# Making two of the four weight sums of a column pair in accumulating DMAs

## The chip, the cores and the metric

The kernel runs on one core of a Trainium2 chip. The metric is the device time of one execution in microseconds. The engines are TensorE (PE in the profile, with its weight loads as PEld), VectorE (DVE), ScalarE (ACT), GpSimd (POOL) and SyncE (SP), which only issues DMAs. GpSimd issues DMAs as well. Each engine runs its instructions strictly in the order of the program.

## The reference

One layer of a hybrid network on 640 tokens (128 of context, 512 latent): a SwiGLU feed-forward half step, a mixer (bidirectional mLSTM and a gated short convolution), and a second half step, all in float32. Cut to the large products:

```python
h = modulate(rmsnorm(x, norm_g[0]), sh1, sc1)
x = x + 0.5 * g1 * swiglu(h, ffn1_w1, ffn1_w2)     # w1: 1024 x 5632, w2: 2816 x 1024
h = modulate(rmsnorm(x, norm_g[1]), shm, scm)
y, C, n, m = mixer(h, C0, n0, m0, ...)             # h @ w_in: 1024 x 9232, then three 1024 x 1024
x = x + gm * y
h = modulate(rmsnorm(x, norm_g[2]), sh2, sc2)
x = x + 0.5 * g2 * swiglu(h, ffn2_w1, ffn2_w2)

def swiglu(h, w1, w2):
    a, b = jnp.split(h @ w1, 2, axis=-1)
    return (jax.nn.silu(a) * b) @ w2
```

## The kernel before

**Exact products.** A float32 operand is split into a rounded high part and the rest: `split` (L75, L79) makes `wh` on ScalarE by a cast and `wl` on VectorE by a subtraction. A product is three matmuls (`three`, L245 to L247): high by high, high by low, low by high, each 128 x 128 weights by 320 tokens.

**Column pairs.** Most large products go two columns of 128 outputs at a time, for the two halves of the tokens (320 each) and the two halves of the inner dimension (512 each). That is a 2 x 2 product of blocks, made with seven products instead of eight in Winograd's form. The seven take the weight operands A11, S1, S2, A12, S3, S4, A22 in this order, with the sums

S1 = A21 + A22, S2 = S1 - A11, S3 = A11 - A21, S4 = A12 - S2.

Of a block Aij, i is the column and j the half of the inner dimension. Each of the seven multiplies by an activation operand of its own, which is kept split as well: 11, T1, T2, 21, T3, 22, T4, in tiles named H11, HT1 and so on, or U where they are made inside the feed-forward. One product is 4 x 3 matmuls. There are 81 pairs. `pair_steps` issues the products and the evacuations between them; among these is the copy of S2's result in PSUM to another bank by ScalarE (L290), where S3's product is then accumulated; VectorE adds partial results (L301).

**Weights.** SP loads the two columns of a pair with one 512 KB DMA each (`w_load`, L202) into the ring `wr` of five tiles. `cast_more` then makes the sums into the ring `ws` (four tiles, L218) and the split operands into the rings `wh` and `wl` (six each), up to four operands ahead of TensorE. The four sums are VectorE's, except that in ten pairs of the mixer (`cx_pair` and `bg_pair`, argument `e1`) S1 and S3 are GpSimd's. A tile of `wr` is free for the next load when its last block is cast (`rdone`).

**The feed-forward** takes its hidden columns in groups of 6 or 8; after each group the product with w2 is added to x. In the second feed-forward two of the groups are "eights": the activation tiles HT3 and HT4 are lent to the hidden values, saved before in DRAM (`h_away`, to `hd`) and read back behind the group's use (`h_back`: 16 DMAs of 160 KB on GpSimd, HT3 before HT4, L981). Each waits until TensorE has read the lent tile for the last time. In between, x itself goes to DRAM and back by `x_away` (L969) and `x_back` (L966), on GpSimd too.

**Order.** The order on each engine is that in which the Python code issues; nothing reorders it. Work for GpSimd stands in its queue wherever a step of the program puts it. A DMA of SP or GpSimd takes one of eight semaphores in turn, and waits until the DMA that used it before has landed.

Of the kernel before, what the change touches and what calls it, by code (L numbers as in the profile page):

```python
# [7 lines left out]
F32 = mybir.dt.float32  # L8
# [36 lines left out]
def mixer_step(ctx: ExitStack, tc: tile.TileContext, x_prompt, x_sample, state_C, state_n, state_m,  # L45
# [33 lines left out]
            V.tensor_sub(lo, raw, f32(hi))  # L79


    RAWB, OPB, SB, AHEAD = 5, 6, 4, 4
    raws, ops = [], []
    rtile, optile, rdone = {}, {}, set()
    ptr = {"dma": 0, "sum": 0, "cast": 0, "use": 0, "held": 0, "hold": False, "cap": 1 << 20}
    fill = []

    def drain(left=0):
        while len(fill) > left:
            fill.pop(0)["emit"]()  # L90

    def load_more(upto=1 << 20):
        while ptr["dma"] < min(upto, len(raws)) and (ptr["dma"] < RAWB or ptr["dma"] - RAWB in rdone):
            n = ptr["dma"]
            rtile[n] = ring.tile([P, 1024], F32, name="wr", bufs=RAWB)
            raws[n](rtile[n])
            ptr["dma"] += 1

    def ready(op):
        return all(r < ptr["dma"] for r in op["raws"])  # L100

    def cast_more(upto):
        load_more()
        while ptr["cast"] < min(upto, ptr["held"] + OPB, ptr["cap"], len(ops)):
            n = ptr["cast"]
            if not ready(ops[n]):
                return
            while ptr["sum"] < min(n + 2, len(ops)) and ready(ops[ptr["sum"]]):
                o = ops[ptr["sum"]]
                o["ap"] = o["src"](o)  # L110
                ptr["sum"] += 1
            o = ops[n]
            w = o["n"]
            hi = ring.tile([P, 512], F32R, name="wh", bufs=OPB)
            lo = ring.tile([P, 512], F32R, name="wl", bufs=OPB)
# [84 lines left out]
    def w_load(w, row0, nk, col0, ncol):  # L200
        def load(t):
            nc.sync.dma_start(t[:, :nk * P].rearrange("p (k n) -> p k n", k=nk),  # L202
                              dap(w, row0 * ncol + col0, [[ncol, P], [P * ncol, nk], [1, P]]))
        return load


# [1 line left out]

    LH, RH = slice(0, 512), slice(512, 1024)

    def pair_ops(r1=0, r2=1, e1=None):
        e1 = e1 or V

        def total(key, engine, fn, a, b):
            def src(o):
                g = o["group"].setdefault(r1, {})
                t = g[key] = ring.tile([P, 512], F32, name="ws", bufs=SB)
                getattr(engine, fn)(t, part(o, a), part(o, b))  # L218
                return t
            return src  # L220

        def part(o, key):
            if key[0] == "S":
                return o["group"][r1][key]
            return rtile[o["base"] + (r1 if key[1] == "1" else r2)][:, LH if key[2] == "1" else RH]

        whole = lambda key: lambda o: part(o, key)
        spec = lambda src, *r: {"raws": list(r), "n": 512, "src": src}
        return {
            "A11": spec(whole("A11"), r1), "A12": spec(whole("A12"), r1), "A22": spec(whole("A22"), r2),  # L230
            "S1": spec(total("S1", e1, "tensor_add", "A21", "A22"), r2),
            "S2": spec(total("S2", V, "tensor_sub", "S1", "A11"), r1, r2),
            "S3": spec(total("S3", e1, "tensor_sub", "A11", "A21"), r1, r2),
            "S4": spec(total("S4", V, "tensor_sub", "A12", "S2"), r1, r2),
        }

    ACT_OF = {"A11": "11", "A12": "21", "A22": "T4", "S1": "T1", "S2": "T2", "S3": "T3", "S4": "22"}
# [29 lines left out]
    def pair_steps(order, ev, spare_v, acts):  # L267
        S = {}

        def prod(name, ps, start):  # L270
            hi, lo = op()
            for kk in range(4):
                three(ps[:, :HT], hi, lo, kk, acts[ACT_OF[name]][kk], start and kk == 0, kk == 3)

        for name in order:
            if name == "A11":
                S["a"] = big()
                prod(name, S["a"], True)
                S["b"] = big()
                A.copy(S["b"][:, :HT], S["a"][:, :HT])  # L280
                flush()
            elif name == "S1":
                e = big()
                prod(name, e, True)
                S["p5"] = t3()
                A.copy(S["p5"], e[:, :HT])
            elif name == "S2":
                prod(name, S["b"], False)
                S["c"] = big()
                A.copy(S["c"][:, :HT], S["b"][:, :HT])  # L290
            elif name == "A12":
                prod(name, S["a"], False)
                ev(0, 0, S["a"][:, :HT])
            elif name == "S3":
                prod(name, S["c"], False)
                S["c22"] = t3()
                if spare_v:
                    A.copy(S["c22"], S["c"][:, :HT])
                    V.tensor_add(S["c22"], S["c22"], S["p5"])
                else:  # L300
                    V.tensor_add(S["c22"], S["c"][:, :HT], S["p5"])  # L301
            elif name == "S4":
                prod(name, S["b"], False)
                V.tensor_add(S["p5"], S["b"][:, :HT], S["p5"])
                ev(0, 1, S["p5"])
            else:
                prod(name, S["c"], False)
                late.append(lambda: ev(1, 0, S["c"][:, :HT]))
                late.append(lambda: ev(1, 1, S["c22"]))
            yield  # L310

    def pair_el(load1, load2, ev, e1=None, spare_v=False, acts=HB, at=None, calm=False):
        po = pair_ops(e1=e1)
# [10 lines left out]
        return dict(element([load1, load2], [po[name] for name in ORDER], emit), pair=True)  # L324

    def tile_ops(nk, t=0):
        out = []
# [565 lines left out]
    def right_chain(n, sh):  # L893
# [26 lines left out]
            V.tensor_sub(N["T", k], N[1, k], N[0, k])  # L920

        def t2(k):
            V.tensor_sub(N["T", k], N[1, k + 4], N["T", k])

        def t3_(k):
            V.tensor_sub(N[1, k], N[1, k + 4], N[1, k])

        def t4(k):
            V.tensor_sub(N["T", k], N[0, k + 4], N["T", k])
# [53 lines left out]
    def eights(w1, w2, g, f0, n_head, head, more, back):  # L983
# [24 lines left out]
        def ev_of(j):  # L1008
            sa, k = {}, j % 4

            def left():
                put_own("11", k, sa[0])

            def diff1():
                V.tensor_sub(raw2(k), raw3(k), sa[0])
                put_own("T1", k, raw2(k))

            def diff2():
                V.tensor_sub(raw2(k), sa[1], raw2(k))
                put_own("T2", k, raw2(k))  # L1020

            def diff3():
                put_own("21", k, sa[0])
                V.tensor_sub(raw3(k), sa[1], raw3(k))

            def diff4():
                put_22(k, sa[1])
                V.tensor_sub(raw2(k), sa[0], raw2(k))

            def ev(mi, h, src):  # L1030
                if mi == 0:
                    sa[h] = raw3(k) if h and j < 4 else t3()
                    A.activation(sa[h], src, AF.Silu)
                    return
                V.tensor_mul(sa[h], src, sa[h])
                if h == 0:
                    if j < 4:
                        lazy.append(left)
                else:
                    lazy.extend([diff1] if j < 4 else [diff2, diff3, diff4])  # L1040
            return ev
# [33 lines left out]
                               spare_v=True, acts=UB, at=at))  # L1075
        return grp, w2s

    def ffn(w1, w2, g, lists, head_of, n_head, e1=None, groups=(6, 6, 6, 4), more={}):

        head, els, f0 = [], [], 0  # L1080
        for gi, size in enumerate(groups):
# [6 lines left out]
            for j in range(size):  # L1088
# [14 lines left out]
                if f0 + j < n_head:  # L1103
                    head.extend(blocks_of(p))
                else:
                    grp.append(pair_el(*p, e1 if f0 == 0 else None, at=more.get(gi, {}).get(j)))
# [777 lines left out]

    h0 = head_q(0)
    chain, work = right_chain(1, SHM)
    prog.append(head_el(blocks_of(h0[0]) + blocks_of(h0[1]), chain, work, mod_mid(GM, 0), gate_rows))
    def tanh_first():
        A.activation(tp.tile([P, 3], F32, name="rstd", bufs=2)[:, 0:1], eps, AF.Tanh)

    prog += [step(spill_x), step(halve), step(tanh_first)]
    cols, gate, NG = gate_cols(), gates(), 22
    h1 = head_q(1)
    first_gml = pair_el(*gml_pair(0), spare_v=True)
# [141 lines left out]
    prog += with_units(ml, mod_dve(GM, (1,), m_wide) + mod_dve(SH2, (1,), m_wide))  # L2036
    for m in range(0, KT, 2):
        if m:
            prog += [pair_el(*cx_pair(m), G), pair_el(*cx_pair(m + 1), G)]
        prog.append(pair_el(*bg_pair(m), G, spare_v=True))  # L2040
# [136 lines left out]
```

## Time and profile before

| | |
|---|---|
| runs | 1652.0, 1652.42, 1652.5 us; median 1652.42 |
| profiled execution | 1651.78 us; its span 1649.9 us |
| TensorE busy | 1628.9 us (99%), 11093 matmuls, granted clock 0.999 |
| VectorE, ScalarE, GpSimd busy | 1319.5 us (80%), 826.4 us (50%), 223.3 us (14%) |
| weight sums | 304 on VectorE (0.684 us each), 20 on GpSimd (1.299 us) |
| DRAM | read 188.98 MB, written 25.79 MB |

The profile is of one execution. A row of the timeline gives the start, the duration, the engine, the line, and the operation with output<-input; in brackets stands how long the engine was idle before it and what released it. Instructions of one engine overlap in the pipeline, so that the distance between two starts is shorter than a duration. A row of the DMA list gives the queue, the number of DMAs, their size and the median time from issue to landing.

### The profile page before, as it was taken

Reading aid. Unit: us, or ns where it says so; the run is one execution under the profiler, and the core shown is the slowest. Engines: PE = TensorE matmul, PEld = TensorE weight load, DVE = VectorE, ACT = ScalarE, POOL = GpSimd, SP = SyncE. Lnnn points to the kernel's source line nnn. Section 1 sums busy time; section 2 is a strip of 40 time slices with the busy share of each in tenths; the row PEclk is TensorE's granted clock in tenths of the full one; section 3 lists DMA queues with packets and bytes.
Section 4 is the critical chain, followed back from the end, with each engine's and each line's share of the span. In section 5 each row is a group of like instructions: output and inputs, shape, how many; then the busy total and the mean of one; then the engine's idle time right before and its main releaser. Section 6 shows DMA issues by size and latency. Waiting matters only on the chain.

```text
span 1649.9 us, 29478 instructions
## 1 busy us (share of the span) xinstructions
PE 1628.9 (99%) x11093; PEld 1585.9 (96%) x11093; DVE 1319.5 (80%) x2786; ACT 826.4 (50%) x1805; POOL 223.3 (14%) x354
## 2 busy tenths in 40 slices
PE   8999999999999999999999999999999999999998
PEld 5999999999999999999999999999999999999997
DVE  6867887887778878788897899779688897898765
ACT  5642542542566655465561455633275555564443
POOL 2010000000031321221121221011112012003002
PEclk9999999999999999999999999999999999999999
DMA  9454343343353433342258432357355256337522
GB/s 321 116 165 120 105 128 112 103 125 94 114 172 102 102 101 90 84 118 71 84 180 263 113 90 78 106 169 222 117 166 141 84 178 175 88 117 219 172 81 64
DMA packets 283661, 216.68 MB, mean 131 GB/s; under 512 B 9331, under 2 KB 260602, under 8 KB 283520
## 3 DMA queue, kind: packets, MB, share of 16 engines
q1 hardware_dynamic: 263152, 158.36, 33.4%
q0 software_dynamic: 20336, 56.45, 11.5%
q8 instruction: 87, 1.43, 0.4%
q14 instruction: 54, 0.44, 0.1%
q10 hardware_dynamic: 32, 0.01, 0.0%
HBM read 188.98 MB, written 25.79 MB: 130 GB/s over the span
## 4 chain that ended last, share of the span: by engine, by line
PE 89%; DVE 4%; ACT 3%; DMA 2%; issue 1%; POOL 0%; SPq 0%; ACTq 0%; DVEq 0%
PE ps L245 27%; PE ps L246 27%; PE ps L247 27%; PE ax L1717 2%; PE ax L1748 2%; PE ax L1720 1%; DVE wl L79 1%; ACT wh L75 1%; ACT Uh L867 1%; DMA early<-in_w_mod_dram 1%; DMA HT4l<-hd 1%; PE ax L1694 1%; DMA wr<-in_ffn_w_dram 0%; ACT Uh L75 0%; DVE Uh L859 0%
## 5 line engine op out<-in xcount | busy, mean ns | idle before, releaser
L79 DVE TENSOR_TENSOR wl<-wr,wh 128x512 fp32r<-128x512 f32 (+1 forms) x389 | 261.4, 684 | 79.8 <-ACT wh L75 77.5
L75 ACT CAST wh<-wr 128x512 fp32r<-128x512 f32 (+1 forms) x391 | 230.2, 600 | 89.1 <-PE ps L246 69.3
L79 DVE TENSOR_TENSOR wl<-ws,wh 128x512 fp32r<-128x512 f32 x324 | 228.0, 704 | 39.5 <-ACT wh L75 38.7
L75 ACT CAST wh<-ws 128x512 fp32r<-128x512 f32 x324 | 199.0, 620 | 108.9 <-DVE ws L218 71.4
L245 PE MATMUL ps<-Uh,wh 128*128 128x320 f32 x576 | 179.8, 312 | 0.0
L246 PE MATMUL ps<-Ul,wh 128*128 128x320 f32 x576 | 177.9, 309 | 0.2
L247 PE MATMUL ps<-Uh,wl 128*128 128x320 f32 x576 | 177.7, 309 | 0.0
L245 PE MATMUL ps<-HT4h,wh 128*128 128x320 f32 x408 | 128.5, 315 | 0.2 <-DVE t L301 0.2
L246 PE MATMUL ps<-HT4l,wh 128*128 128x320 f32 x408 | 126.3, 309 | 0.5 <-DMA HT4l<-hd 0.4
L247 PE MATMUL ps<-HT4h,wl 128*128 128x320 f32 x408 | 126.0, 309 | 0.0
L245 PE MATMUL ps<-H11h,wh 128*128 128x320 f32 x376 | 118.8, 316 | 0.7 <-ACT H11h L75 0.7
L245 PE MATMUL ps<-H21h,wh 128*128 128x320 f32 x376 | 117.7, 313 | 0.0
L246 PE MATMUL ps<-H11l,wh 128*128 128x320 f32 x376 | 116.5, 310 | 0.3
L247 PE MATMUL ps<-H21h,wl 128*128 128x320 f32 x376 | 116.2, 309 | 0.0
L247 PE MATMUL ps<-H11h,wl 128*128 128x320 f32 x376 | 116.1, 309 | 0.0
L246 PE MATMUL ps<-H21l,wh 128*128 128x320 f32 x376 | 116.0, 308 | 0.0
L245 PE MATMUL ps<-HT3h,wh 128*128 128x320 f32 x356 | 112.0, 315 | 3.5 <-ACT ps L290 3.5
L246 PE MATMUL ps<-HT3l,wh 128*128 128x320 f32 x356 | 110.0, 309 | 0.0
L247 PE MATMUL ps<-HT3h,wl 128*128 128x320 f32 x356 | 110.0, 309 | 0.0
L245 PEld LDWEIGHTS ps<-Uh,wh 128*128 128x128 f32 x576 | 108.1, 188 | 1.4 <-issue 0.8
L246 PEld LDWEIGHTS ps<-Ul,wh 128*128 128x128 f32 x576 | 108.1, 188 | 0.7 <-DVE Ul L79 0.7
L247 PEld LDWEIGHTS ps<-Uh,wl 128*128 128x128 f32 x576 | 108.1, 188 | 0.0
(477 smaller groups left out, 4699.4 us busy)
## 6 DMA issues: line engine op xcount, KB each, us to landing
wr<-in_ffn_w_dram SPq DMA_DIRECT2D x102, 512.0 KB, 3.9
wr<-in_w_in_dram SPq DMA_DIRECT2D x72, 512.0 KB, 3.9
wr<-in_w_mod_dram SPq DMA_DIRECT2D x51, 512.0 KB, 3.9
wr<-in_ffn_w_dram SPq DMA_DIRECT2D x32, 384.0 KB, 3.3
xd<-x POOLq DMA_DIRECT2D x32, 320.0 KB, 5.4
x<-xd POOLq DMA_DIRECT2D x32, 320.0 KB, 4.0
early<-in_w_mod_dram SPq DMA_DIRECT2D x13, 512.0 KB, 9.0
mg<-in_w_mod_dram POOLq DMA_DIRECT2D x8, 512.0 KB, 5.6
```

Of the source, the lines that this page charges most:

```text
L75: A.copy(hi, raw)
L79: V.tensor_sub(lo, raw, f32(hi))
L245: PE.matmul(ps, hi[:, ws], ah, start=start, stop=False, skip_group_check=True)
L246: PE.matmul(ps, hi[:, ws], al, start=False, stop=False, skip_group_check=True)
L247: PE.matmul(ps, lo[:, ws], ah, start=False, stop=stop, skip_group_check=True)
L867: A.activation(t[:, a:b], t[:, a:b], AF.Identity, scale=sc_, bias=bi_)
L1694: PE.matmul(p[:, :P], S["k", dt][:, sl], S["q", dt][:, sl], start=(dt == 0), stop=(dt == 1))
L1717: PE.matmul(p2[:, :DH + 1], S["q", dt][:, sl], S["C"][d][:, dt, :], start=(dt == 0), stop=(dt == 1))
L1720: PE.matmul(p1[:, :DH + 1], S["p", ch][:, d, :], PO["vt"][:, ch, :], start=True, stop=True)
L1748: PE.matmul(p[:, :DH + 1], kw[:, dt * P:(dt + 1) * P], PO["vt"][:, ch, :], start=True, stop=True)
```

## The change

S1 = A21 + A22 and S3 are no longer computed by an engine. For each pair SP loads the block A21 twice, into the two halves of a `wr` tile (`sums`), then the first column (A11, A12) as before, then the block A22 into a new ring `wq` of two half-size tiles (`last`). GpSimd then issues two DMAs with `accum_op=add` (`more`): A22 onto one copy of A21, which makes S1, and A11 onto the other, which makes S3 = A11 + A21. Each waits for the landing of its plain copy. `add_more` emits them, at the start of the next `cast_more`, or just ahead of a sum that needs them. For this S3 has to be a sum; so signs change elsewhere: S2 = S1 + A11 and S4 = A12 + S2, the activation operands T2 and T3 are negated and T4, made from T2, adds it, VectorE subtracts S4's result where it added it, and the copy of S2's result (L290) becomes a ScalarE activation with scale -1. S2 and S4 stay on VectorE; the ring `ws` shrinks to two tiles. The argument `e1` is gone. The step `spill_x` (DMAs of x to DRAM) moves ahead of the head element of the mixer.

```diff
-    RAWB, OPB, SB, AHEAD = 5, 6, 4, 4
+    RAWB, HALFB, OPB, SB, AHEAD = 5, 2, 6, 2, 4
...
+    turns, accs = {"wr": [], "wq": []}, []
...
     def load_more(upto=1 << 20):
-        while ptr["dma"] < min(upto, len(raws)) and (ptr["dma"] < RAWB or ptr["dma"] - RAWB in rdone):
+        while ptr["dma"] < min(upto, len(raws)):
             n = ptr["dma"]
-            rtile[n] = ring.tile([P, 1024], F32, name="wr", bufs=RAWB)
+            kind = getattr(raws[n], "kind", "wr")
+            seq, bufs = turns[kind], RAWB if kind == "wr" else HALFB
+            if len(seq) >= bufs and seq[-bufs] not in rdone:
+                return
+            seq.append(n)
+            rtile[n] = ring.tile([P, 1024 if kind == "wr" else 512], F32, name=kind, bufs=bufs)
             raws[n](rtile[n])
+            if hasattr(raws[n], "more"):
+                accs.append((n, raws[n].more))
             ptr["dma"] += 1
+
+    def add_more(n=1 << 20):
+
+        while accs and accs[0][0] <= n:
+            r, f = accs.pop(0)
+            f(rtile[r])
...
     def cast_more(upto):
+        add_more()
         load_more()
...
+                add_more(max(o["raws"]))
...
-    def pair_ops(r1=0, r2=1, e1=None):
...
+    def pair_loads(load1, load2):
+
+        def quad(t, o, load, half, queue, **kw):
+            w, row0, col0, ncol = load.src
+            queue.dma_start(t[:, 512 * o:512 * o + 512].rearrange("p (k n) -> p k n", k=4),
+                            dap(w, (row0 + 512 * half) * ncol + col0, [[ncol, P], [P * ncol, 4], [1, P]]), **kw)
+
+        def sums(t):
+            for o in (1, 0):
+                quad(t, o, load2, 0, nc.sync)
+
+        def more(t):
+            quad(t, 1, load2, 1, G, accum_op=OP.add)
+            quad(t, 0, load1, 0, G, accum_op=OP.add)
+
+        def last(t):
+            quad(t, 0, load2, 1, nc.sync)
+        sums.more = more
+        last.kind = "wq"
+        return [sums, load1, last]
...
-            "S1": spec(total("S1", e1, "tensor_add", "A21", "A22"), r2),
-            "S2": spec(total("S2", V, "tensor_sub", "S1", "A11"), r1, r2),
-            "S3": spec(total("S3", e1, "tensor_sub", "A11", "A21"), r1, r2),
-            "S4": spec(total("S4", V, "tensor_sub", "A12", "S2"), r1, r2),
+            "A11": spec(whole("A11"), 1), "A12": spec(whole("A12"), 1), "A22": spec(whole("A22"), 2),
+            "S1": spec(whole("S1"), 0), "S3": spec(whole("S3"), 0),
+            "S2": spec(total("S2", "S1", "A11"), 0, 1),
+            "S4": spec(total("S4", "A12", "S2"), 1),
...
-                A.copy(S["c"][:, :HT], S["b"][:, :HT])
+                A.activation(S["c"][:, :HT], S["b"][:, :HT], AF.Copy, scale=-1.0)
...
-                V.tensor_add(S["p5"], S["b"][:, :HT], S["p5"])
+                V.tensor_sub(S["p5"], S["b"][:, :HT], S["p5"])
...
             def diff2():
-                V.tensor_sub(raw2(k), sa[1], raw2(k))
+                V.tensor_sub(raw2(k), raw2(k), sa[1])
...
+    prog.append(step(spill_x))
     prog.append(head_el(blocks_of(h0[0]) + blocks_of(h0[1]), chain, work, mod_mid(GM, 0), gate_rows))
...
-    prog += [step(spill_x), step(halve), step(tanh_first)]
+    prog += [step(halve), step(tanh_first)]
...
-            prog += [pair_el(*cx_pair(m), G), pair_el(*cx_pair(m + 1), G)]
+            prog += [pair_el(*cx_pair(m)), pair_el(*cx_pair(m + 1))]
```

What this does to the order is shown at one place of the second feed-forward, the second return of HT3 and HT4 (at 1513 us in the profile before). In a row stand the line, the operation and the tiles with their numbers (`wr` a tile of weights, `xd` and `hd` the copies of x and of HT3 and HT4 in DRAM, `in_ffn2_w1_dram` the weights there); x2 means twice in a row. GpSimd before:

```order
L969 DMA xd_133<-x_15067 128x640
L966 DMA x_15066<-xd_133 128x640
L966 DMA x_15067<-xd_133 128x640
L969 DMA xd_133<-x_15064 128x640
L969 DMA xd_133<-x_15065 128x640
L981 DMA HT3h_18684<-hd_134 128x320
L981 DMA HT3l_18685<-hd_134 128x320
```

GpSimd in the changed kernel:

```order
L1004 DMA x_15128<-xd_133 128x640
L232 DMA wr_18565<-in_ffn2_w1_dram 128x4x128 x2
L1007 DMA xd_133<-x_15125 128x640
L1007 DMA xd_133<-x_15126 128x640
L232 DMA wr_18712<-in_ffn2_w1_dram 128x4x128 x2
L1019 DMA HT3h_18770<-hd_134 128x320
L1019 DMA HT3l_18771<-hd_134 128x320
```

Two accumulating DMAs (L232) stand between the last save of x and the first of the 16 returns; at the first return it is the same. SP before, around the load that it issues at 1510.8 us:

```order
L202 DMA wr_18605<-in_ffn2_w1_dram 128x8x128
L202 DMA wr_18627<-in_ffn2_w1_dram 128x8x128
L202 DMA wr_18781<-in_ffn2_w1_dram 128x8x128
L202 DMA wr_18803<-in_ffn2_w1_dram 128x8x128
L202 DMA wr_18940<-in_ffn2_w1_dram 128x8x128
```

SP in the changed kernel, around the plain copies onto which those two accumulate:

```order
L232 DMA wr_18565<-in_ffn2_w1_dram 128x4x128 x2
L218 DMA wr_18666<-in_ffn2_w1_dram 128x8x128
L232 DMA wq_18710<-in_ffn2_w1_dram 128x4x128
L232 DMA wr_18712<-in_ffn2_w1_dram 128x4x128 x2
L218 DMA wr_18843<-in_ffn2_w1_dram 128x8x128
```

The copies for a pair (`wr_18712`, L232, twice) stand behind the A22 load of the pair before (`wq_18710`), which needs one of the two `wq` tiles.

More of the change, by code (lines that the diff above doesn't have):

```diff
@@ L203, in load, with pair_ops, total @@
                               dap(w, row0 * ncol + col0, [[ncol, P], [P * ncol, nk], [1, P]]))
+        load.src = (w, row0, col0, ncol)
         return load
     LH, RH = slice(0, 512), slice(512, 1024)
-    def pair_ops(r1=0, r2=1, e1=None):
-        e1 = e1 or V
-        def total(key, engine, fn, a, b):
+    def pair_loads(load1, load2):
[14 more added lines that the diff above has]
+        return [sums, load1, last]
+    def pair_ops():
+        def total(key, a, b):
             def src(o):
-                g = o["group"].setdefault(r1, {})
-                t = g[key] = ring.tile([P, 512], F32, name="ws", bufs=SB)
-                getattr(engine, fn)(t, part(o, a), part(o, b))
+                t = o["group"][key] = ring.tile([P, 512], F32, name="ws", bufs=SB)
+                V.tensor_add(t, part(o, a), part(o, b))
                 return t
             return src
+        AT = {"S3": (0, LH), "S1": (0, RH), "A11": (1, LH), "A12": (1, RH), "A22": (2, slice(0, 512))}
         def part(o, key):
-            if key[0] == "S":
-                return o["group"][r1][key]
-            return rtile[o["base"] + (r1 if key[1] == "1" else r2)][:, LH if key[2] == "1" else RH]
+            if key not in AT:
+                return o["group"][key]
+            r, sl = AT[key]
+            return rtile[o["base"] + r][:, sl]
         whole = lambda key: lambda o: part(o, key)
@@ L229, in pair_ops @@
         return {
-            "A11": spec(whole("A11"), r1), "A12": spec(whole("A12"), r1), "A22": spec(whole("A22"), r2),
-            "S1": spec(total("S1", e1, "tensor_add", "A21", "A22"), r2),
-            "S2": spec(total("S2", V, "tensor_sub", "S1", "A11"), r1, r2),
-            "S3": spec(total("S3", e1, "tensor_sub", "A11", "A21"), r1, r2),
-            "S4": spec(total("S4", V, "tensor_sub", "A12", "S2"), r1, r2),
+            "A11": spec(whole("A11"), 1), "A12": spec(whole("A12"), 1), "A22": spec(whole("A22"), 2),
+            "S1": spec(whole("S1"), 0), "S3": spec(whole("S3"), 0),
+            "S2": spec(total("S2", "S1", "A11"), 0, 1),
+            "S4": spec(total("S4", "A12", "S2"), 1),
         }
@@ L310, in pair_steps, with pair_el @@
             yield
-    def pair_el(load1, load2, ev, e1=None, spare_v=False, acts=HB, at=None, calm=False):
-        po = pair_ops(e1=e1)
+    def pair_el(load1, load2, ev, spare_v=False, acts=HB, at=None, calm=False):
+        po = pair_ops()
         at = at or {}
@@ L323, in emit @@
                     f()
-        return dict(element([load1, load2], [po[name] for name in ORDER], emit), pair=True)
+        return dict(element(pair_loads(load1, load2), [po[name] for name in ORDER], emit), pair=True)
     def tile_ops(nk, t=0):
@@ L922, in t2 @@
         def t2(k):
-            V.tensor_sub(N["T", k], N[1, k + 4], N["T", k])
+            V.tensor_sub(N["T", k], N["T", k], N[1, k + 4])
         def t3_(k):
-            V.tensor_sub(N[1, k], N[1, k + 4], N[1, k])
+            V.tensor_sub(N[1, k], N[1, k], N[1, k + 4])
         def t4(k):
-            V.tensor_sub(N["T", k], N[0, k + 4], N["T", k])
+            V.tensor_add(N["T", k], N[0, k + 4], N["T", k])
         ks = range(4)
@@ L1023, in diff3 @@
                 put_own("21", k, sa[0])
-                V.tensor_sub(raw3(k), sa[1], raw3(k))
+                V.tensor_sub(raw3(k), raw3(k), sa[1])
             def diff4():
                 put_22(k, sa[1])
-                V.tensor_sub(raw2(k), sa[0], raw2(k))
+                V.tensor_add(raw2(k), sa[0], raw2(k))
             def ev(mi, h, src):
@@ L1076, in eights, with ffn @@
         return grp, w2s
-    def ffn(w1, w2, g, lists, head_of, n_head, e1=None, groups=(6, 6, 6, 4), more={}):
+    def ffn(w1, w2, g, lists, head_of, n_head, groups=(6, 6, 6, 4), more={}):
         head, els, f0 = [], [], 0
@@ L1105, in ffn @@
                 else:
-                    grp.append(pair_el(*p, e1 if f0 == 0 else None, at=more.get(gi, {}).get(j)))
+                    grp.append(pair_el(*p, at=more.get(gi, {}).get(j)))
             acts = lambda k, h, U=U: U[k, h]
@@ L2038, in mixer_step @@
         if m:
-            prog += [pair_el(*cx_pair(m), G), pair_el(*cx_pair(m + 1), G)]
-        prog.append(pair_el(*bg_pair(m), G, spare_v=True))
+            prog += [pair_el(*cx_pair(m)), pair_el(*cx_pair(m + 1))]
+        prog.append(pair_el(*bg_pair(m), spare_v=True))
     prog += weave([pair_el(*gsc_pair(m)) for m in range(0, KT, 2)], [step(lambda: None)] * 3 + [step(t_in(0))])
```

## The prediction

> **What bounds the kernel now.** I read the page first (span, busy shares, the chain that ended last), then what TensorE waits for, then GpSimd's and TensorE's timeline where those waits and the edited instructions meet. From the page:
>
> ```profile
> span 1649.9 us, 29478 instructions
> PE 1628.9 (99%) x11093; PEld 1585.9 (96%) x11093; DVE 1319.5 (80%) x2786; ACT 826.4 (50%) x1805; POOL 223.3 (14%) x354
> PE 89%; DVE 4%; ACT 3%; DMA 2%; issue 1%; POOL 0%; SPq 0%; ACTq 0%; DVEq 0%
> ```
>
> TensorE is busy 99% of the span and carries 89% of the chain. The edit leaves its instructions as they are, so the time changes only by what is added to or taken from its waits. The profiled execution took 1651.78 us: the span plus 1.88 us around it, and 0.64 below the median of 1652.42; I make the sum against 1651.78 and give the forecast against the median. The waits that touch pair elements are these (total, times, longest):
>
> ```profile
> PE ps L245 <- ACT ps L290: 3.5, 4, 2.2
> PE ps L245 <- ACT H11h L75: 0.7, 1, 0.7
> PE ps L246 <- DMA HT4l<-hd: 0.4, 1, 0.4
> PE ps L245 <- ACT ps L280: 0.4, 1, 0.4
> PE ps L245 <- DVE t L301: 0.2, 1, 0.2
> ```
>
> That is 5.2 us in all: the ceiling of any gain, however much VectorE is relieved. No row has TensorE wait for a weight sum or for a pair's weights from DRAM.
>
> **The sums taken off VectorE and GpSimd.** The weight sums as they are:
>
> ```profile
> L218 DVE TENSOR_TENSOR ws<-wr x142: 672/684/1170, 62.9 to 1580.1; 128x512 f32<-128x512 f32 x142
> L218 DVE TENSOR_TENSOR ws<-ws,wr x81: 657/684/693, 64.1 to 1574.7; 128x512 f32<-128x512 f32 x81
> L218 POOL TENSOR_TENSOR ws<-wr x20: 1283/1299/1682, 904.9 to 1020.0; 128x512 f32<-128x512 f32 x20
> ```
>
> S1 and S3 are the 142 on VectorE and the 20 on GpSimd; S2 and S4 (81 each) stay. How far does this reach TensorE? Its longest wait, 2.22 us, and another with VectorE behind it:
>
> ```profile
> 1285.24 0.49 DVE L79 TENSOR_TENSOR Ul<-x,Uh 128x320 fp32r<-128x320 f32 x1 [0.53 <-ACT Uh L75]
> 1286.17 0.46 ACT L75 CAST Uh<-x 128x320 fp32r<-128x320 f32 x1 [0.96 <-DVE x L1019]
> 1288.24 0.41 PE L245 MATMUL ps<-HT3h,wh 128*128 128x320 f32 x1 [2.22 <-ACT ps L290]
> 1289.28 0.68 DVE L218 TENSOR_TENSOR ws<-wr 128x512 f32<-128x512 f32 x1
> 1289.88 0.68 DVE L79 TENSOR_TENSOR wl<-wr,wh 128x512 fp32r<-128x512 f32 x1
> 1291.71 0.31 PE L247 MATMUL ps<-H22h,wl 128*128 128x320 f32 x1
> 1292.22 0.41 PE L245 MATMUL ps<-HT4h,wh 128*128 128x320 f32 x1 [0.20 <-DVE t L301]
> ```
>
> The first is a ping-pong: VectorE waits for ScalarE (0.53), ScalarE for VectorE (0.96), over activation splits that the edit keeps. There is no S1 or S3 in it, and I leave it standing. The second has an S3 sum in VectorE's unbroken run just ahead; from its start to the next instruction's is 0.60 us, so the run to L301 shortens by more than the hole in TensorE's row, 1292.22 - 1291.71 less one matmul interval of 0.15 (1628.9 us over 11093 matmuls), or 0.36 us. That goes. The wait on L280 has such a sum at the head of an unbroken run of VectorE too, 8 us earlier:
>
> ```profile
> 71.16 0.69 DVE L218 TENSOR_TENSOR ws<-wr 128x512 f32<-128x512 f32 x1
> 80.47 0.41 PE L245 MATMUL ps<-HT2h,wh 128*128 128x320 f32 x1 [0.37 <-ACT ps L280]
> ```
>
> With the handover behind the 0.37 I take 0.5. Gain: 0.4 + 0.5 = 0.9 us. The other 142 x 0.60 = 85 us of VectorE, and the 20 x 1.3 = 26 us of GpSimd, are idle time that nobody waits for. The bounds of the gain are 0 and the 5.2 above.
>
> **Signs and the scaled copy.** Subtractions for additions have one price: the sums above take 684 ns either way. The 81 copies of S2's product become activations with scale -1:
>
> ```profile
> 1287.77 0.41 ACT L290 COPY ps<-ps 128x320 f32<-128x320 f32 x1
> 1462.40 0.44 ACT L1033 ACTIVATE t<-ps 128x320 f32<-128x320 f32 x1 [0.53 <-PE ps L247]
> ```
>
> That is 0.03 us more each, 2.4 us of an engine at 50%. The result is needed only after A12's twelve matmuls, 12 x 0.15 = 1.8 us later; without that cover it would cost up to those 2.4 us.
>
> **The new DMAs.** Per pair: 1.75 MiB read where 1.0 was, 81 x 0.75 MiB = 63.7 MB on the page's 188.98 MB; SP issues four DMAs for two, GpSimd two accumulating ones, 162 in all. Nothing here shows an accumulating DMA, so its landing is bounded by these (KB each, us to landing):
>
> ```profile
> wr<-in_ffn_w_dram SPq DMA_DIRECT2D x12, 256.0 KB, 3.3
> C<-in_state_C_dram POOLq DMA_DIRECT2D x8, 256.0 KB, 3.1
> mg<-in_w_mod_dram POOLq DMA_DIRECT2D x8, 512.0 KB, 5.6
> early<-in_w_mod_dram SPq DMA_DIRECT2D x13, 512.0 KB, 9.0
> ```
>
> Below: 3.1, as for a plain 256 KB. Above: 9.0, twice the bytes in a crowded stretch. I take 5, near the 512 KB row, because the destination has to be read as well. Issuing: GpSimd spent 0.54 us on a 128-row DMA (below), 0.95 on one with 1024 rows; this has 512, so I take 0.8.
>
> ```profile
> 105.60 0.95 POOL L1474 DMA_DIRECT2D gw<-in_w_in_dram  x1
> ```
>
> The Trainium skill, "Collectives: The Full Stack", on why ReduceScatter is half of AllGather, says that an add in the DMA engines fetches two sources over one ring and so moves at half the rate. No run shown has such a DMA; by that rule a landing of 5.6 (the 512 KB row) would replace my 5.
>
> In the steady pairs this is in time:
>
> ```profile
> 1437.90 0.37 SPq L202 DMA_DIRECT2D wr<-in_ffn_w_dram  x1
> 1463.17 0.63 ACT L75 CAST wh<-ws 128x512 fp32r<-128x512 f32 x1 [0.33 <-DVE ws L218]
> ```
>
> The load leaves 25 us ahead of the cast of that pair's S1: 0.4 + 3.3 (plain copy) + 0.8 + 5 (accumulate) take 9.5, and some 15 us stay. Two buffers for A22, and sums of a pair that queue behind them on SP, use up part of it; at the tightest pairs, by the same prices and the order, I estimate that 5 us are left. GpSimd's own tensor work slides later behind the accumulates; the modulation weights at the start and the mLSTM masks have, by the same count, the room. Cost of all that: 0; with accumulates over 10 us each the cover is gone.
>
> **Where it collides: the return of HT3 and HT4.** In FFN2 the 16 DMAs of h_back wait on GpSimd for TensorE to release the buffers, and then run back to back. Twice:
>
> ```profile
> 1364.65 0.54 POOL L981 DMA_DIRECT2D HT3h<-hd  x1 [4.11 <-PE ps L247]
> 1372.92 0.56 POOL L981 DMA_DIRECT2D HT4l<-hd  x1
> DMA to landing us min/median/max: 6.4/6.4/6.4
> 1381.03 0.31 PE L246 MATMUL ps<-HT4l,wh 128*128 128x320 f32 x1
> 1513.34 0.54 POOL L981 DMA_DIRECT2D HT3h<-hd  x1 [4.13 <-PE ps L247]
> 1521.19 0.64 POOL L981 DMA_DIRECT2D HT4l<-hd  x1
> DMA to landing us min/median/max: 9.0/9.0/9.0
> 1530.28 0.42 PE L246 MATMUL ps<-HT4l,wh 128*128 128x320 f32 x1 [0.39 <-DMA HT4l<-hd]
> ```
>
> The last HT4l lands at 1372.92 + 6.4 = 1379.3 the first time, and TensorE reads it at 1381.03: 1.7 us to spare. The second time it lands at 1521.19 + 9.0 = 1530.2, and TensorE stands already: none to spare.
>
> In the changed order two accumulates stand directly ahead of these 16. They wait for their plain copies, which leave SP behind the A22 load, and that load needs a buffer that VectorE frees at the same moment as a raw buffer before:
>
> ```profile
> 1362.12 0.37 SPq L202 DMA_DIRECT2D wr<-in_ffn_w_dram  x1
> 1510.82 0.37 SPq L202 DMA_DIRECT2D wr<-in_ffn_w_dram  x1
> 1517.00:1521.00 4.00, 4.00 (x29) 4.00 (x29) 4.00 (x9) 1.57 (x3) 4.00 (x9) 1.00 1.15 263
> ```
>
> So 1510.82 + 0.37 + 3.3 (copy landed) + 2 x 0.8 = 1516.1 is where h_back starts: 2.8 us late. (The first time 1362.12 + 5.27 = 1367.4, also 2.8 late.) The bounds by issue price alone (0.54 to 0.95 each) are 2.2 and 3.1. The last row, a window, shows the DMA engines full there (share 1.15, 263 GB/s). The accumulates bring 0.5 MiB, another 0.5 if the destination is read, and the sums 0.25 more: at 263 GB/s 1 to 5 us, of which only what is ahead of HT4 in the queues counts. I add 1.2, for 4.0 us late. A second path gives the same size: a GpSimd DMA takes one of eight semaphores in turn and waits for the one eight before it, so the seventh DMA of h_back waits for the first accumulate, issued at 1514.5: with a landing of 5 after 0.8 of issue at 1520.3, where 1516.5 was its time (six steps of 0.52 behind the first), 3.8 late. At a landing of 9 it is 7.8 late.
>
> Loss: 4.0 - 1.7 = 2.3 the first time, 4.0 the second, 6.3 together. Nothing hides it: those matmuls are next in TensorE's order.
>
> **Sum.** +6.3 - 0.9 = +5.4 us: 1657.2 against the profiled 1651.78, 1657.8 against the median. With lateness d the sum is 2d - 2.6: 1.8 at d = 2.2, 13.0 at d = 7.8. By the rule cited above d would be 4.4 and the sum 6.2.
>
> **Rivals.**
> - *The relief reaches all of TensorE's waits, faster.* If the ping-pong at 1285 starts earlier because VectorE has less ahead of it, up to the 4.8 us of the ACT and DVE rows go: 1652.4 - 4.8 = 1647.6, provided h_back isn't late. It decides if A22's buffer comes free 3 us sooner, so that the accumulates are issued before 1513.3. Against it: VectorE's 0.53 gap just there, which shows it waiting, not behind. Chance 0.09.
> - *The return is hidden after all, no change.* The 9.0 us to land, against 3.1 for a like DMA at rest, is backlog. If SP's other loads move ahead into the 2.8 us in which h_back stands, HT4 lands about when it did: d = 2 at the first place (0.3 lost) and 1 to 2 at the second, less 0.9: 1652 to 1655. For it: the full window; against it: the extra bytes. Chance 0.28.
> - *Slow accumulates, clearly slower.* At 10 us to land, the seventh return goes at 1525.3, 8.8 late: 2 x 8.8 - 2.6 = 15, 1667, and the tightest steady pairs begin to wait. For it: 512-byte rows and two reads; against it: no GpSimd DMA row near that. Chance 0.13.
>
> **How the numbers follow.** The forecast has 0.50: 1657.8, its own range 1655 to 1662 by d from 3 to 6. The bound for "no change" is 0.2%, 3.3 us, about what this measurement can tell: 1649.1 to 1655.7. Slower: nearly all of the 0.50 and the 0.13, 0.62; same: the hidden return and the low edge of the forecast, 0.29; faster 0.09. The range for 8 in 10, 1650.5 to 1667, leaves out most of the faster case and half of the slow one.
>
> **What would show it.** Right: the waits of TensorE gain a row on HT4l (or HT4h, HT3) from hd of 4 to 8 us in two times; h_back's first DMA starts some 3 us after TensorE released its buffer, with the two accumulates just ahead; VectorE falls to about 1235 us, GpSimd's 20 sums are gone, DRAM reads rise to 252.7 MB, and the 3.5 us on L290 stay. Wrong: no late return (then the order of release differs from what I read), a wait of TensorE for casts of S1 or S3, or an accumulating DMA that costs GpSimd several us to issue.

## The result: 25 us slower, and where they went

The changed kernel takes 1677.92 us (1677.08 to 1679.18) beside 1652.46 us for the kernel before on the same chip: a ratio of 1.0154, 95% interval 1.0136 to 1.0172. The direction was forecast, the size was not: 1657.8 was the forecast, 1667 the upper end of the range.

The page of the changed kernel (span; busy time; DRAM):

```profile
span 1677.4 us, 29946 instructions
PE 1642.5 (98%) x11093; PEld 1594.1 (95%) x11093; DVE 1227.2 (73%) x2644; ACT 820.5 (49%) x1805; POOL 407.2 (24%) x496
HBM read 252.68 MB, written 25.79 MB: 166 GB/s over the span
```

VectorE lost the 142 sums and 92 us, GpSimd's busy time grew by 184 us, and the bytes are those foreseen. TensorE has the same 11093 matmuls, in the same order. So the start of each can be set beside its start before, and the growth of the distance shows where the 27.6 us between the two profiled executions went:

| place (time before) | later by, us | forecast, us |
|---|---|---|
| 79.8 and 1291.7, the two waits behind a sum on VectorE | -0.54, -0.36 | -0.9 |
| mixer, 586 to 601 | +3.3 | 0 |
| mixer, 788 to 796 | +4.2 | 0 |
| mixer, 864 (run 1 has 0.4 of it too) and 919 | +1.0 | 0 |
| 1286 to 1310, half clock behind an old wait | +1.4 | 0 |
| first return of HT3 and HT4, 1376 | +8.3 | +2.3 |
| second return, 1525 to 1530 | +10.1 | +4.0 |
| all else | +0.2 | 0 |

The waits of TensorE (total, times, longest) answer to it; left out are those at the start of the kernel, which were there before:

```profile
PE ps L283 <- DMA HT3h<-hd: 8.3, 4, 4.9
PE ps L283 <- ACT ps L328: 3.5, 4, 2.2
PE ax L1732 <- ACT kw L1745: 2.3, 1, 2.3
PE ps L283 <- ACT ps L318: 1.4, 1, 1.4
PE ax L1755 <- ACT Cc L1791: 1.0, 1, 1.0
```

The 3.5 us on ScalarE's copy of S2's result stand as before, as foreseen: no relief of VectorE reaches them. New are the returns and three waits in the mixer.

**The second return.** Timeline of the changed kernel, by engine: SP issues the A22 load and the two plain copies; GpSimd the two accumulates and h_back; TensorE reads HT3. The lines on landing are, in this order, for the plain copies (the trace has the landing of the second alone) and the four HT3h:

```profile
1528.37 0.37 SPq L232 DMA_DIRECT2D wq<-in_ffn_w_dram  x1
1528.84 1.30 SPq L232 DMA_DIRECT2D wr<-in_ffn_w_dram  x2
DMA to landing us min/median/max: 8.3/8.3/8.3
1537.52 2.68 POOL L232 DMA_DIRECT2D wr<-in_ffn_w_dram  x2 [7.08 <-DMA wr<-in_ffn_w_dram]
1539.09 1.69 POOL L1019 DMA_DIRECT2D HT3h<-hd  x1
1546.88 0.54 POOL L1019 DMA_DIRECT2D HT3l<-hd  x1 [2.87 <-DMA wr<-in_ffn_w_dram]
DMA to landing us min/median/max: 8.1/8.5/8.7
1547.37 0.61 PE L283 MATMUL ps<-HT3h,wh 128*128 128x320 f32 x1 [4.91 <-DMA HT3h<-hd]
```

All is 17.55 us later than before at this point. So the A22 load at 1528.37 is exactly where the prediction had it (1510.82 + 17.55), and so is the pace of the accumulates: 1539.09 - 1537.52 = 2 x 0.79 us. But the copies landed after more than 8 us instead of 3.3. GpSimd waited at their accumulate for 7.08 us, and h_back began at 1539.09, 8.2 us later than 1513.34 + 17.55 = 1530.89. Then its first HT3h took 8.1 us to land, and its eighth DMA waited 2.87 us for the semaphore of the second accumulate. TensorE therefore stood already at HT3, which is read two products, 3.5 us, ahead of HT4. The first return shows the same: 7.4 us late. All eight HT3h of the two returns, before and then in the changed kernel:

```profile
HT3h<-hd POOLq DMA_DIRECT2D x8, 160.0 KB, 3.2
HT3h<-hd POOLq DMA_DIRECT2D x8, 160.0 KB, 8.2
```

**The mixer.** GpSimd and ScalarE of the changed kernel, then ScalarE before:

```profile
580.29 1.33 POOL L232 DMA_DIRECT2D wr<-in_w_in_dram  x1 [4.68 <-DVE t L342]
583.22 1.87 POOL L1692 TENSOR_TENSOR wt<-mask,wt 128x256 f32<-128x256 bf16 x2
584.48 0.70 ACT L1698 ACTIVATE wt<-wt,colT 128x128 f32<-128x128 f32 x2 [3.92 <-POOL wt L1692]
588.15 0.42 PE L283 MATMUL ps<-HT2h,wh 128*128 128x320 f32 x1 [1.43 <-ACT ps L318]
792.82 0.69 ACT L1698 ACTIVATE wt<-wt,colT 128x128 f32<-128x128 f32 x2 [3.09 <-POOL wt L1692]
```

```profile
580.48 0.68 ACT L1660 ACTIVATE wt<-wt,colT 128x128 f32<-128x128 f32 x2
```

The mask product `wt` of the mLSTM stands behind an accumulate in GpSimd's queue. Before, ScalarE had it at 580.48; now it waits 3.92 us for it, ScalarE's copy of a pair's result in PSUM stands behind that on ScalarE, and TensorE waits for the copy. (The profile puts the accumulate's wait of 4.68 us down to an instruction of VectorE that ended near that time; the second plain copy landed at 581.6, and the second accumulate follows it.) At 789 us GpSimd stands 9.06 us before an accumulate whose copies had left SP only at 784.45 and took 4.4 us to land. The next masks come late, ScalarE waits 3.09 us for them (last row of the first view) and makes `kw`, another tile of the mLSTM, behind them, and TensorE waits 2.3 us for `kw`. Most of the rest at this place, 1.6 us, is TensorE at half its clock behind that wait. I had given all this room and a cost of 0.

### The profile page after: what moved, and what is told of

It reads as the page before. It is cut to its first block, busy times and chain, and to the rows that moved or that the text cites. A ratio compares the mean times of both kernels' runs of the same rounds, so it can differ in the third digit from the quotient of the medians.

```text
span 1677.4 us, 29946 instructions
## 1 busy us (share of the span) xinstructions
PE 1642.5 (98%) x11093; PEld 1594.1 (95%) x11093; DVE 1227.2 (73%) x2644; ACT 820.5 (49%) x1805; POOL 407.2 (24%) x496
## 4 chain that ended last, share of the span: by engine, by line
PE 41%; DMA 3%; issue 3%; DVE 2%; ACT 2%; POOL 0%; SPq 0%; ACTq 0%; DVEq 0%; POOLq 0%
PE ps L283 13%; PE ps L284 13%; PE ps L285 13%; DMA wr<-in_ffn_w_dram 2%; DMA HT3l<-hd 1%; DVE wl L79 1%; DMA wr<-in_w_in_dram 1%; ACT wh L75 1%; DMA x<-rd 0%; PE ax L2106 0%; DVE x L745 0%; ACT Uh L75 0%; ACT Uh L905 0%; PE ax L1786 0%; PE ax L754 0%
## 5 line engine op out<-in xcount | busy, mean ns | idle before, releaser
L79 DVE TENSOR_TENSOR wl<-wr,wh 128x512 fp32r<-128x512 f32 x470 | 319.5, 689 | 140.9 <-ACT wh L75 138.1
L75 ACT CAST wh<-wr 128x512 fp32r<-128x512 f32 x472 | 274.8, 600 | 113.2 <-PE ps L284 75.5
L232 POOL DMA_DIRECT2D wr<-in_ffn_w_dram x94 | 122.5, 1493 | 508.0 <-DMA wr<-in_ffn_w_dram 285.2
L232 POOL DMA_DIRECT2D wr<-in_w_in_dram x68 | 89.1, 1486 | 278.1 <-DMA wr<-in_w_in_dram 87.2
L79 DVE TENSOR_TENSOR wl<-ws,wh 128x512 fp32r<-128x512 f32 x162 | 111.6, 689 | 27.1 <-ACT wh L75 26.5
L75 ACT CAST wh<-ws 128x512 fp32r<-128x512 f32 x162 | 100.7, 622 | 39.8 <-DVE ws L254 30.0
L991 DVE SCALAR_TENSOR_TENSOR x<-ps,modT,x 128x128 f32<-128x128 f32 (+2 forms) x176 | 66.0, 423 | 61.1 <-PE ps L285 53.7
```

The source lines that it names most:

```text
L75: A.copy(hi, raw)
L232: queue.dma_start(t[:, 512 * o:512 * o + 512].rearrange("p (k n) -> p k n", k=4), dap(w, (row0 + 512 * half) * ncol + col0, [[ncol, P], [P ...
L991: V.scalar_tensor_tensor(x[:, o + a:o + b], ps[:, a:b], modT[:, g, m, cd:cd + 1], x[:, o + a:o + b], op0=OP.mult, op1=OP.add)
```

## The experiments

Two theories. W: an accumulate stands at the head of GpSimd's queue until its plain copy has landed, and what is queued behind waits with it. T: the accumulating traffic itself, dearer for the DMA engines than plain traffic, makes everything land late. The kernels of one group ran on one chip beside the kernel before (1652.36 us for the first four, 1652.45 for the others).

**1. No accumulates** (`more` left empty).

```diff
         def more(t):
-            quad(t, 1, load2, 1, G, accum_op=OP.add)
-            quad(t, 0, load1, 0, G, accum_op=OP.add)
+            pass
```

> The changed kernel without its 162 accumulating DMAs; their terms A22 and A11 are missing from S1 and S3, and the plain copies, the sign changes and the order of everything else stay. Both theories lay the loss on the accumulates, so both expect the time of before or 1 us less: 1651 to 1654 us, no wait of TensorE for HT3 or HT4 over 0.5 us, none for kw at 790 us. If the 18 MB or so of extra plain copies, the two wq tiles or the moved step spill_x were the cause, 1660 us or more.

1650.54 us, ratio 0.9991 (0.9982 to 1.0001), half a microsecond below the range that both theories gave and far from 1660; among TensorE's waits is none for HT3, HT4 or `kw`. So the plain copies (21.2 MB more read in this run, rather than the 18 expected), the signs, the `wq` ring and the moved spill_x cost nothing that can be seen. It is also the ceiling of this form of the idea, 1.8 us below the kernel before: with VectorE at 74% instead of 80%, this is all that relieving it brings.

**2. Plain DMAs at the same place.**

```diff
-            quad(t, 1, load2, 1, G, accum_op=OP.add)
-            quad(t, 0, load1, 0, G, accum_op=OP.add)
+            quad(t, 1, load2, 1, G)
+            quad(t, 0, load1, 0, G)
```

> The 162 DMAs stay at their place on GpSimd, with the same wait for the landing of the copy under them, but they overwrite instead of adding, so that S1 and S3 hold A22 and A11 alone. Theory W (they stand at the head of GpSimd's queue and wait for their copies, and what is queued behind waits with them): most of the loss stays, 1668 to 1676 us, the return of HT3 still starts 5 us or more late. Theory T (an accumulating DMA costs the DMA engines twice the time of a plain one, and this backlog delays the returns): most of the loss goes, 1653 to 1662 us.

1665.86 us, ratio 1.0083 (1.0068 to 1.0098): between the two expectations, 15.3 us over the run without and 12.1 under the changed kernel. The wait is there, and h_back starts 6.1 and 5.6 us late, as W expected (row of GpSimd at the second return; the copies' landing):

```profile
1527.80 1.51 POOL L232 DMA_DIRECT2D wr<-in_ffn_w_dram  x2 [7.31 <-DMA wr<-in_ffn_w_dram]
DMA to landing us min/median/max: 5.4/5.4/5.4
```

The copies land after 5.4 us rather than 8.3. So neither theory holds alone, and the next runs separate them.

**3. The returns ahead of the accumulates.** `add_more` holds back from the last save of x to the end of the returns:

```diff
-        while accs and accs[0][0] <= n:
+        while accs and not (ptr.get("back") and n == 1 << 20) and accs[0][0] <= n:
...
+                if m + 2 == KT:
+                    at[1] = at[1] + [lambda: ptr.update(back=True)]
...
-                    at[6] = [lambda: h_back("T4")] if back else []
+                    at[6] = [lambda: h_back("T4"), lambda: ptr.update(back=False)] if back else []
```

> The changed kernel, but at the two returns of HT3 and HT4 the pending pair of accumulates is issued behind the 16 returns instead of ahead of them; nothing else moves. W: 13 to 18 of the 18.4 us lost there come back and the 8 us in the mixer stay: 1660 to 1665 us, the first HT3 return issued within 1 us of TensorE's release. T: the returns still land late in the crowded DMA engines, 1668 us or more.

1664.66 us, ratio 1.0074 (1.0059 to 1.0089), as W expected. h_back starts as soon as TensorE releases HT3, at both returns (the second here):

```profile
1520.56 0.54 POOL L1019 DMA_DIRECT2D HT3h<-hd  x1 [0.26 <-PE ps L285]
```

The two returns cost 1.6 and 2.8 us instead of 8.3 and 10.1; the mixer lost 5.7 us in this execution. With h_back on time, the 4.4 us left at the returns go with late landings: HT3h lands 5.4 to 8.6 us after issue (2.5 to 4.1 before), and at the second return the sixth DMA of h_back waits 2.30 us for an accumulate's semaphore. That is T's share there.

**4. All accumulates five products later.**

```diff
-                accs.append((n, raws[n].more))
+                accs.append((n, raws[n].more, ptr["use"] + 5))
...
-    def add_more(n=1 << 20):
+    def add_more(n=None):
...
-        while accs and accs[0][0] <= n:
-            r, f = accs.pop(0)
+        while accs and (accs[0][2] <= ptr["use"] if n is None else accs[0][0] <= n):
+            r, f, _ = accs.pop(0)
```

> Every pair of accumulates is issued five products (some 9 us) later in GpSimd's order, unless a cast needs it sooner; the bytes are the same. W: by then the copies have landed, so hardly anything waits on GpSimd: the losses in the mixer and at both returns go, 1651 to 1656 us. T: the same bytes in the same stretches, 1665 us or more.

1654.50 us, ratio 1.0015 (1.0006 to 1.0025), as W expected: 23.4 of the 25.5 us come back with every byte still moved. What it loses against the run without accumulates, 4.0 us in the medians and 5.4 in the profiled executions, is 1.7 us at 594 to 601 (TensorE behind ScalarE's `Cc`, behind GpSimd's store of it), 0.8 from 919 to 1000, and 2.5 at the returns, the rest in small pieces.

**5. The wait alone.** Each accumulate shrinks to 16 bytes a partition, with its wait:

```diff
-            quad(t, 1, load2, 1, G, accum_op=OP.add)
-            quad(t, 0, load1, 0, G, accum_op=OP.add)
+            for o, load, half in ((1, load2, 1), (0, load1, 0)):
+                w, row0, col0, ncol = load.src
+                G.dma_start(t[:, 512 * o:512 * o + 4], dap(w, (row0 + 512 * half) * ncol + col0, [[ncol, P], [1, 4]]))
```

> The changed kernel with each accumulating DMA replaced by one of 16 bytes a partition at the same place, which overwrites and waits for the same copy: the wait stays, nearly all of the 85 MB of accumulating traffic goes, and the sums are not made. If the wait is long only because the accumulates' own bytes hold up the copies, the copies land in the 4.1 us of the run without accumulates, h_back starts 3 to 4 us late, and the prediction's own sum comes out: 1655 to 1661 us. If the wait is as long without the bytes: 1668 us or more. If waiting by itself costs nothing: 1650 to 1653 us.

1659.44 us, ratio 1.0043 (1.0027 to 1.0060), within the range of the prediction's own sum. The second return in it (SP's copies and their landing, GpSimd's small DMAs, h_back):

```profile
1516.65 1.00 SPq L232 DMA_DIRECT2D wr<-in_ffn_w_dram  x2
DMA to landing us min/median/max: 3.9/3.9/3.9
1520.72 1.13 POOL L242 DMA_DIRECT2D wr<-in_ffn_w_dram  x2 [6.75 <-ACT wh L75]
1521.85 0.55 POOL L1020 DMA_DIRECT2D HT3h<-hd  x1
```

The first copy lands at about 1520.6 (the profile puts the wait down to a cast of ScalarE that ended near that time), and h_back starts 3.2 us late, where the prediction had 2.8. The two returns cost 2.3 and 1.9 us, 4.2 together where the prediction had 6.3. So the lateness is the forecast one, but that the time fits as well is in part luck: in the profiled execution the mixer adds 1.7 us, and two stretches at half the clock of TensorE add 1.2 (at 31 us) and 1.5 (at 1291), none of which was in the sum.

The mixer in this run shows that a wait of GpSimd need not cost anything. At the place of 789 us it is as long as in the changed kernel. But the copies leave SP 1.4 us earlier against TensorE's progress, and GpSimd is through the two DMAs and the two masks behind them in 2.5 us rather than 4.0, so that ScalarE waits 0.45 us for the masks (3.09 there) and TensorE not at all:

```profile
786.66 1.11 POOL L242 DMA_DIRECT2D wr<-in_w_in_dram  x2 [9.09 <-DMA wr<-in_w_in_dram]
788.51 0.70 ACT L1699 ACTIVATE wt<-wt,colT 128x128 f32<-128x128 f32 x2 [0.45 <-POOL wt L1693]
```

**6. Accumulates in the mixer only.**

```diff
         def more(t):
+            if load1.src[0] is not w_in:
+                return
```

> Accumulates only in the 34 pairs of the mixer's input weights; in the 47 pairs of the feed-forwards they are left out, and S1 and S3 lack a term there. W, with the mixer's loss made by GpSimd's own work (masks, state) queued behind the waiting accumulates: the 8 us in the mixer stay and those at the two returns go, 1656 to 1660 us. If the mixer lost its time to something that the feed-forward's accumulates left behind: 1653 us or less.

1657.30 us, ratio 1.0030 (1.0018 to 1.0042): 6.8 us over the run without accumulates, and in its profile the mixer is 6.0 us later than before and the returns lose nothing. So the mixer's loss is of its own making, by the accumulates in it.

**7. Nine products later** (9 for 5 in the diff of run 4).

> As five_later, but nine products (some 16 us) later. If what five_later still lost (4 us against the run without accumulates) is waiting that is left, 1651 to 1653 us; if it is traffic, no change, 1653.5 to 1656 us; if the sums now come too late for their casts, 1658 us or more.

1660.84 us, ratio 1.0050 (1.0035 to 1.0065). The time is in the third range. At the second return the accumulates now stand behind x's return, and the casts wait for them, which costs 2.2 us. GpSimd, then VectorE, ScalarE and TensorE:

```profile
1539.94 5.24 POOL L232 DMA_DIRECT2D wr<-in_ffn_w_dram  x4 [0.66 <-issue]
1548.63 0.69 DVE L254 TENSOR_TENSOR ws<-wr 128x512 f32<-128x512 f32 x1 [3.17 <-DMA wr<-in_ffn_w_dram]
1548.68 0.62 ACT L75 CAST wh<-wr 128x512 fp32r<-128x512 f32 x1 [2.71 <-DMA wr<-in_ffn_w_dram]
1550.48 0.41 PE L283 MATMUL ps<-HT4h,wh 128*128 128x320 f32 x1 [1.45 <-DVE t L339]
```

That is not the whole: of the 10.9 us between the profiled executions of run 1 and of this run, 5.2 lie at the two returns, where h_back starts on time but HT3h lands 7.0 to 7.8 us after issue, and 1.5 at half the clock at 1291 us.

**Taken together**, in medians against the run without accumulates (1650.54):

| | few waits on GpSimd | waits for the copies |
|---|---|---|
| no or few bytes | 0 (run 1) | +8.9 (run 5) |
| plain bytes | not run | +15.3 (run 2) |
| accumulating bytes | +4.0 (run 4) | +27.4 (the change) |

Waiting alone costs 8.9, the bytes alone 4.0, both together 27.4, far more than the sum of the two. The bytes lengthen the landing for which GpSimd stands still (3.9, 5.4, 8.3 us in runs 5, 2 and the change), and what stood still is then issued into the crowd. Two things are mixed into these figures. Stretches at half clock are in them, 2.7 us in the profiled execution of run 5, at least 5.1 in that of the change, none (before the last 10 us) in those of runs 1 and 4. And GpSimd itself is busy longer with an accumulate (1.3 us each over run 1's busy time; 0.75 for a plain DMA, 0.5 for one of 16 bytes a partition); no run separates this from the traffic. No version beats the kernel before: the ceiling is 1.8 us, within the noise, and run 4 stays 2 us above the kernel before.

## Why the prediction was wrong

- **The gain** of 0.9 us was right in place and size: -0.54 at 79.8, -0.36 at 1291.7. The ping-pong at 1285 was rightly left standing.
- **The collision** was rightly named: the two accumulates ahead of h_back, held by copies that go out behind the A22 load, at the times forecast.
- **The step that failed at the returns** is "1510.82 + 0.37 + 3.3 (copy landed)". The 3.3 is the median of twelve loads before 445 us, none in this stretch, while the same paragraph quotes the window with the DMA engines at 1.15. At this place the copies take 4.1 us without accumulates (run 1). I added the extra bytes only once, 1.2 us, behind h_back's start, and not to the landing that sets its start. Copies: 8.3 us for 3.3. Lateness: 7.4 and 8.2 us for 2.8. With these the prediction's own terms give 7.4 - 1.7 and 8.2, 13.9 us at the returns; measured are 18.4. HT3h's own landing grew too (8.2 us in the median, 3.2 before), and with the slack of HT4 alone in view (1.7 and 0) I missed that HT3 would be late first. Run 5, which takes the bytes away, gives back the lateness forecast (3.2).
- **The step that failed in the mixer** is "Cost of all that: 0": I weighed whether the accumulates come in time for their casts, which they do, and gave a sentence to what stands behind them on GpSimd. Masks and the state's store do; 8.4 us here, 5.7 and 6.0 in runs 3 and 6. GpSimd was busy 14%, but its order, not its busy time, was the resource. How much each accumulate may delay there is a matter of slack, which I did not work out: run 5 has the waits and loses 1.7 us in the mixer.
- **A term that the sum did not have** is the half clock of TensorE behind the new waits, at least 5.1 us in the profiled execution (last section).
- **The accumulate's own landing**, taken as 5 us, was about right in the median (5.8 and 5.1), though the two at the second return took 4.8 and 8.3; the issue price was right (0.8 for 0.79). The changed kernel's DMA list:

```profile
wr<-in_ffn_w_dram POOLq DMA_DIRECT2D x94, 256.0 KB, 5.8
wr<-in_w_in_dram POOLq DMA_DIRECT2D x68, 256.0 KB, 5.1
```

Run 2's plain ones, at the same places, landed after 3.9 and 3.5 us.

- **The rival of slow accumulates** had the right size at the returns (15 us forecast, 18.4 measured) mostly for another reason: it had the accumulates land after 10 us, and what set the start of h_back was the plain copy ahead of them. Its path is there too, but smaller: the 2.87 us for which the eighth DMA of the second return waited on an accumulate. It had 0.13; it should have had more, since every extra byte lengthened the wait.

## What to carry to other kernels

A DMA that must wait for another DMA, on a queue that serves other work in order, costs what stands behind it, however idle the engine: list what follows it in that queue, and put it there only after its wait is over (five products later gave 92% of the loss back), but not so late that its result is waited for (nine products later gave back less). Price a landing from the stretch where it will happen, with the change's own bytes in it, not from a median over the program. Work taken off an engine at 80% is worth only the waits of the bounding engine that end on it; here 0.9 us of 92.

## What the runs showed of the hardware

**The accumulating DMAs here take 2.3 times the DMA time of plain ones.** GpSimd's queue in the changed kernel, in run 2 and in run 1 (packets, MB, share of 16 engines' span):

```profile
q0 software_dynamic: 105872, 98.92, 32.0%
```

```profile
q0 software_dynamic: 33296, 98.92, 20.4%
```

```profile
q0 software_dynamic: 20336, 56.45, 11.5%
```

For the same 162 DMAs of 256 KB that is 0.320 x 1677.4 - 0.115 x 1648.3 = 347 us of all 16 engines accumulating and 0.204 x 1664.2 - 190 = 150 us plain: 2.14 and 0.93 us each, 122 and 283 GB/s. (This is the time that packets took; it can hold waiting, as the shares of up to 1.30 in the windows below show.) The packets differ as well: 528 for each accumulate, 80 for each plain DMA of the same shape. The Trainium skill, "Collectives: The Full Stack", on why ReduceScatter is half of AllGather, has an add in the DMA engines fetch two sources over one ring and so move at half the rate; the 2.3 of these traces is near that, and somewhat more.

**TensorE's clock halves behind a wait.** The changed kernel in windows at the first return (columns: PE, PEld, DVE, ACT and POOL busy, granted clock, DMA share, GB/s), and two matmuls behind the second return:

```profile
1385.00:1390.00 5.00, 2.08 (x9) 1.15 (x7) 1.95 (x3) 1.46 (x3) 2.99 (x6) 0.96 1.23 279
1390.00:1395.00 5.00, 3.81 (x10) 2.40 (x10) 0.00 (x0) 0.00 (x0) 3.16 (x6) 0.50 1.30 347
1395.00:1400.00 5.00, 5.00 (x31) 5.00 (x30) 2.48 (x5) 1.50 (x3) 3.80 (x5) 0.85 0.99 259
1553.06 0.47 PE L283 MATMUL ps<-H22h,wh 128*128 128x320 f32 x1
1553.33 0.47 PE L284 MATMUL ps<-H22l,wh 128*128 128x320 f32 x1
```

The interval is 0.27 us instead of 0.147 until the clock is back. In this execution 43 matmuls on 320 tokens ran at that interval while the clock was at half (none in the profiled execution of the kernel before), which makes 43 x 0.12 = 5.1 us, and I had it in no term.

At 1294 us the old wait of 2.2 us on ScalarE, which left the clock at 1.00 before, was followed by the half clock here and in runs 2, 5 and 7, but not in runs 1, 3, 4 and 6. The traces show what decides between them. In each of the nine, the clock changes only at multiples of 3.413 us from its first change (the half-clock stretches of the changed kernel start at 795.73, 1297.49, 1389.65 and 1546.66 us, and the distances from the first are 147, 174 and 220 times 3.413). Where the wait falls nearly whole into one slot of this grid, so that TensorE is busy 1.18 to 1.33 us of it, the next slot is at half (four executions of four); where it is divided between two slots, each with TensorE busy 1.88 us or more, the clock stays (five of five). The two slots of the changed kernel, then two of the kernel before, columns as above:

```profile
1294.08:1297.49 3.41, 1.18 (x8) 0.92 (x7) 2.89 (x8) 2.75 (x7) 0.00 (x0) 1.00 0.26 43
1297.49:1300.90 3.41, 3.41 (x15) 3.41 (x14) 3.26 (x6) 1.26 (x3) 0.00 (x0) 0.50 0.49 141
1283.84:1287.25 3.41, 2.17 (x15) 1.91 (x14) 2.36 (x7) 1.54 (x4) 0.00 (x0) 1.00 0.00 0
1287.25:1290.67 3.42, 2.43 (x16) 2.43 (x17) 3.42 (x8) 2.44 (x6) 0.00 (x0) 1.00 0.04 11
```

Where the slots fall against the program differs from one execution to the next, so this cost is a matter of luck. A threshold for other places is not shown: in run 6 a slot with TensorE busy 1.76 us (at 790.63) left the clock whole, in run 7 one with 2.28 us (at 1533.51) was followed by half.

The Trainium skill, "TensorE: Matmul & The Clock Gate", Part 1, has the clock at half after at least one idle window of about 3.4 us, and its table has only the two rates; the two rates and the length are those of these traces, but the slots that were followed by half at this wait were not idle: TensorE was busy for 35 to 39% of them.
